# Off-diagonal blocks of the chunk inverses: four column groups of 32 instead of block-diagonal 128-wide products, with a new set of ordering numbers

## The chip, the cores and the metric

The kernel runs on one core of a Trainium2 chip. The metric is device time in microseconds (us) of one execution. The kernel before took 1522.41 us (median of 3 runs, 1519.56 to 1522.49). Engines are named as in the profile: PE multiplies matrices (PEld is its weight load), DVE, ACT and POOL work on vectors, SP issues the DMAs.

## What is computed

One layer of a hybrid decoder over 1024 prompt tokens and 8 sample tokens of width 1024: an input projection to 9360 columns, a gated linear attention branch (4 heads), an RWKV-7 branch (16 heads of 64), two up-projections merged by gates, an output projection, and a layer norm. The change lies in the RWKV-7 branch, whose recurrence is

```python
def step(S, inp):                       # S: [value, key] per head
    rt, wt, kt, vt, kkt, at = inp
    sa = jnp.einsum('bhvk,bhk->bhv', S, -kkt)
    S = S * wt[:, :, None, :] + sa[..., None] * (kkt * at)[:, :, None, :] + vt[..., None] * kt[:, :, None, :]
    y = jnp.einsum('bhvk,bhk->bhv', S, rt)
    return S, y
S, ys = lax.scan(step, S0, xs)
```

The projection around it is `p = jnp.einsum('btd,dn->btn', x, w_in)`, and the rest of the layer is

```python
m = (jax.nn.sigmoid(gate_a) * jnp.einsum('btc,cd->btd', o_gla, w_up_gla)
     + jax.nn.sigmoid(gate_b) * jnp.einsum('btc,cd->btd', o_rwkv, w_up_rwkv))
out = jnp.einsum('btd,de->bte', m, w_out)
y_out = _layernorm(DEEPNORM_ALPHA * x + out, ln_g, ln_b, LN_EPS)
```

## The kernel before

**Staging.** The prompt is handled in two passes of 512 tokens; the first also carries the 8 sample tokens. In each pass the weights stream by in blocks of 128 output columns (the big projections write the PSUM tile `proj`); each float32 product is made of three products in a rounded format (high by high, low by high, high by low: tiles `xh`, `xl` of the activations and `wpart` of the weights). Products between plain float32 tiles are recorded by the trace as two matmuls each, except transposes.

**One pair of heads.** The RWKV branch goes by pairs of heads, 8 in each pass, 16 in all. For a pair, `front` makes the chunk matrices: the 512 tokens are cut into `NCH = 8` chunks of `C = 64`, and for each chunk and head a unit-triangular 64 by 64 matrix has to be inverted. The two 32 by 32 diagonal blocks of each are inverted on POOL by 31 steps of elimination (tiles `X` and `Xt`; the operand comes back from DRAM as tile `wide<-LD`), written to DRAM (`XD`) and fetched into tile `XT` by DMAs. The off-diagonal block is (one diagonal inverse) times (the off-diagonal block of the matrix) times (the other diagonal inverse). `back` makes it in two products:

- Step one. Four DVE transposes bring one diagonal inverse of all 16 chunk-head blocks to tile `Xt` (128 partitions = 4 groups of 32, four blocks side by side). Tile `L1` (named `L` in the profile) has zeros but for one 32 by 32 block in each row group. Four matmuls of 128 by 128 weights and 32 moving columns write `pA`. Four copies of 32 partitions bring it to tile `As`, in blocks among zeros.
- Step two. Four matmuls with `As` as weights and 64 columns of `XT` write `pZ`; four copies put it into `XT`.

Then `turn` transposes some operands and `chain` walks through the 8 chunks with four dependent products each (PSUM tiles `pch` and `pY`).

**What sets the order.** Each activity (a pair, a head of the other branch, the block loop, the loads) is a Python generator that yields one instruction at a time. `Order.run` picks the next one by a table of costs (`price`), delays between engines (`HOP`, `SPARE`, `LANDED`), and precedences (`PRIO`, `FOR_PE`, `STAND`). Work that two engines can do goes to the one that the table says ends first, with penalties (`BIAS` for DVE against ACT, `ASIDE` for POOL). The result is one fixed order for each engine. `together` issues several matmuls as one piece. `KEEP` is how many free `row` tiles some requests must leave, and `AHEAD` is how many weight blocks before a change of activations the new activations begin to load. All matmuls, copies and DMAs are issued through the same helper, so nearly all rows of the profile bear L224.

PE can be used as one array (in the profile 128\*128, rows by columns), as two of 64 rows (64\*128: the products `big<-az,wide` in `front`), or as four groups of 32 columns (128\*32). Before, the last form is used only in `gla_sample`, for 8 products of the sample tokens with 256 moving columns, each on four groups (`big<-row 128*32`).

Of the kernel before, what the change touches and what calls it, by code (L numbers as in the profile page):

```python
# [20 lines left out]
P = 128  # L21
# [11 lines left out]
C = 64  # L33
# [15 lines left out]
    "Xt": ([P, P], 1), "S": ([P, GDV], 2), "Sp": ([P, C], 2), "s0p": ([P, C], 2), "rh": ([P, P], 2),  # L49
# [7 lines left out]
KEEP = 2  # L57
AHEAD = 3
# [6 lines left out]
SPARE_ROWS = 7  # L65
EARLY_GATES = 8


HOP = {"P": 0.2, "D": 0.26, "G": 0.14, "V": 0.14, "A": 0.14}
# [5 lines left out]
AGE = 0.5  # L75
# [3 lines left out]
BIAS = 0.145  # L79
ASIDE = 1.145  # L80

PRIO = {"evacuate": 0.7, "pair": 0.3, "turn": 0.5, "chain": 0.5, "norm": 0.1, "x": 0.56, "lora": 0.08, "rank":
        -0.15, "head": 0.3, "gate": -0.18, "w": 0.3, "out": -0.01, "state": 0.16, "block": 0.09}
FOR_PE = {"pair": 1.0, "turn": 1.11, "chain": 1.0, "norm": 0.76, "lora": 0.41, "rank": 1.0, "head": 1.0, "gate": 1.0,
        "state": 1.0, "out": 0.05}
STAND, SCARCE, PER_ROW = 0.042, 0.2, 0.036
# [63 lines left out]
def price(eng, name, out, args, ins):  # L150
# [277 lines left out]
class Kern(Order):  # L428
# [71 lines left out]
    def setup(self):  # L500
# [68 lines left out]

        for tag, n, bufs in (("az", 4 * HT, 2), ("XT", 2 * HT, 2), ("L1", HT, 1), ("As", HT, 1)):  # L570
# [556 lines left out]
    def front(self, c, p, st, d):  # L1127
# [118 lines left out]
        d.AZ, d.BK, d.G, d.XT, d.v, d.bonus, d.pc, d.L, d.L1 = AZ, BK, GG, XT, st[2], st[1], pc, L_, L1  # L1246
        d.y = Pc_[:, :HT]

    def back(self, d):
# [3 lines left out]
        As_, X1_ = (yield from self.get("As")), (yield from self.get("Xt"))  # L1253
        As = As_.rearrange("p (x t) -> p x t", t=P)
        X1 = X1_.rearrange("p (x t) -> p x t", t=32)
# [12 lines left out]
        pZ = yield from self.bank("big", [P, H, 2, 32])  # L1268
        for x in range(H):
            yield self.P.matmul(pZ[:, x], As[:, x], XT[:, x, :, 32:64], start=True, stop=True)  # L1270
        for h in range(2):
            for n in range(2):
                yield self.C.copy(XT[q[2 * h], H * n:H * n + H, h, 32:64], pZ[q[2 * h + n], :, h])
# [3 lines left out]
        self.free(pZ, As_)  # L1277
# [518 lines left out]
```

## Time and profile before

| What | us |
|---|---|
| Median of 3 runs | 1522.41 |
| The profiled execution | 1520.7 |
| Its span, first to last instruction | 1518.9 |
| PE busy | 1502.7 |
| PEld busy | 1348.3 |
| DVE busy | 1092.3 |
| ACT busy | 853.0 |
| POOL busy | 395.1 |

The mean granted clock of PE was 0.999. Rows of the grouped views read: line, engine, operation, output<-inputs, the array's form, partitions by elements, count, busy us, mean ns of one, and the idle time of the engine just before. Rows of the view in order of time read: start, duration, engine, operation, count, and in brackets the idle time before. A matmul's duration is its way through the array and overlaps those of its neighbours; what it costs the stream is the distance from its start to the next start.

### The profile page before, as it was taken

Reading aid. Unit: us, or ns where it says so; the run is one execution under the profiler, and the core shown is the slowest. Engines: PE = TensorE matmul, PEld = TensorE weight load, DVE = VectorE, ACT = ScalarE, POOL = GpSimd, SP = SyncE. Lnnn points to the kernel's source line nnn. Section 1 sums busy time; section 2 is a strip of 40 time slices with the busy share of each in tenths; the row PEclk is TensorE's granted clock in tenths of the full one; section 3 lists DMA queues with packets and bytes.
Section 4 is the critical chain, followed back from the end, with each engine's and each line's share of the span. In section 5 each row is a group of like instructions: output and inputs, shape, how many; then the busy total and the mean of one; then the engine's idle time right before and its main releaser. Section 6 shows DMA issues by size and latency. Waiting matters only on the chain.

```text
span 1518.9 us, 29410 instructions
## 1 busy us (share of the span) xinstructions
PE 1502.7 (99%) x10100; PEld 1348.3 (89%) x10100; DVE 1092.3 (72%) x2306; ACT 853.0 (56%) x2107; POOL 395.1 (26%) x1161
## 2 busy tenths in 40 slices
PE   9999999999999999999999999999999999999997
PEld 8899999999999998888888888888888898897786
DVE  6687596868786698757738695979577746675565
ACT  5556666676576566554746554465567645643210
POOL 2060516051503224052332505051451050000000
PEclk9999999999999999999999999999999999999999
DMA  8777776788677866664455456646574876786332
GB/s 297 261 266 239 269 228 222 239 273 263 203 239 255 289 225 191 217 204 138 153 173 166 126 178 198 207 127 219 181 219 142 247 246 230 260 273 205 128 112 84
DMA packets 206641, 318.45 MB, mean 210 GB/s; under 512 B 87075, under 2 KB 102572, under 8 KB 206492
## 3 DMA queue, kind: packets, MB, share of 16 engines
q1 hardware_dynamic: 206492, 316.56, 64.7%
q8 instruction: 81, 1.33, 0.3%
q14 instruction: 68, 0.56, 0.1%
HBM read 196.82 MB, written 118.61 MB: 208 GB/s over the span
## 4 chain that ended last, share of the span: by engine, by line
PE 94%; DVE 3%; DMA 1%; issue 1%; ACT 0%; SPq 0%; POOL 0%; POOLq 0%; DVEq 0%; ACTq 0%
PE proj L224 58%; PE big L224 21%; PE pY L224 9%; PE pch L224 6%; DVE row L224 1%; DMA wide<-LD 0%; DMA row<-o_gla 0%; DVE wide L224 0%; DVE wpart L224 0%; DVE xl L224 0%; DMA wraw<-w_in 0%; SPq L224 0%; DVE part L224 0%; ACT xh L224 0%; DVE pc L224 0%
## 5 line engine op out<-in xcount | busy, mean ns | idle before, releaser
L224 PE MATMUL proj<-xh,wpart 128*128 128x264 f32 (+2 forms) x3728 | 918.3, 329 | 1.0 <-DVE row L224 1.0
L224 PEld LDWEIGHTS proj<-xh,wpart 128*128 128x128 f32 x3728 | 623.1, 189 | 49.2 <-issue 4.2
L224 PE MATMUL proj<-xl,wpart 128*128 128x264 f32 (+2 forms) x1864 | 614.5, 330 | 0.4 <-DVE xl L224 0.4
L224 PEld LDWEIGHTS proj<-xl,wpart 128*128 128x128 f32 x1864 | 352.1, 189 | 22.2 <-DVE xl L224 1.7
L224 POOL TENSOR_TENSOR Xt<-X,wide 128x60 f32<-128x60 f32 (+24 forms) x496 | 163.7, 330 | 441.1 <-DMA wide<-LD 298.3
L224 DVE TENSOR_TENSOR wpart<-wraw,wpart 128x512 fp32r<-128x512 f32 x209 | 145.5, 698 | 73.4 <-ACT wpart L224 67.4
L224 ACT CAST wpart<-wraw 128x512 fp32r<-128x512 f32 x210 | 130.6, 623 | 98.7 <-PE proj L224 53.4
L224 DVE TENSOR_TENSOR row<-row 128x512 f32<-128x512 f32 (+10 forms) x331 | 173.3, 533 | 8.0 <-ACT row L224 2.2
L224 POOL TENSOR_TENSOR X<-X,Xt 128x60 f32<-128x60 f32 (+24 forms) x496 | 162.6, 328 | 38.8
L224 ACT ACTIVATE row<-row 128x512 f32<-128x512 f32 (+4 forms) x229 | 138.5, 612 | 29.0 <-DVE row L224 19.6
L224 ACT ACTIVATE s0p<-wide,pc 64x64 f32<-64x64 f32 x256 | 88.2, 345 | 34.6 <-DVE wide L224 30.0
L224 DVE SCALAR_TENSOR_TENSOR wide<-pch,pc,s0p 64x64 f32<-64x64 f32 x224 | 62.9, 281 | 59.9 <-PE pch L224 55.2
L224 ACT COPY wide<-pch 64x64 f32<-64x64 f32 x220 | 45.6, 207 | 107.3 <-PE pch L224 103.7
L224 POOL TENSOR_TENSOR row<-row 128x256 f32<-128x256 f32 (+4 forms) x38 | 36.3, 961 | 266.6 <-DVE row L224 187.6
L224 ACT ACTIVATE row<-proj,omu 128x256 f32<-128x256 f32 (+1 forms) x97 | 53.3, 550 | 73.6 <-PE proj L224 70.3
L224 DVE SCALAR_TENSOR_TENSOR row<-proj,pv,row 128x255 f32<-128x255 f32 (+1 forms) x97 | 55.6, 573 | 42.4 <-ACT tail L224 30.3
L224 PE MATMUL big<-row 128*128 128x128 f32 (+3 forms) x456 | 83.6, 314 | 0.0
L224 PE MATMUL big<-xh,wpart 128*128 128x256 f32 (+2 forms) x304 | 73.7, 327 | 0.6 <-ACT xh L224 0.6
L224 POOL TENSOR_SCALAR XT<-XT,st 128x256 f32<-128x256 f32 x1 | 1.2, 1227 | 272.7 <-ACT st L224 272.7
L406 ACT ACT_TABLE_LOAD x50 | 64.2, 1283 | 0.9
L224 DVE COPY rh<-pch 128x128 f32<-128x128 f32 x128 | 37.1, 290 | 37.2 <-PE pch L224 34.9
L224 PEld LDWEIGHTS big<-row 128*128 128x128 f32 (+2 forms) x456 | 58.8, 176 | 5.0 <-ACT row L224 0.6
(253 smaller groups left out, 2526.9 us busy)
## 6 DMA issues: line engine op xcount, KB each, us to landing
w<-wpart SPq DMA_DIRECT2D x146, 512.0 KB
wpart<-w SPq DMA_DIRECT2D x146, 512.0 KB
wraw<-w_in SPq DMA_DIRECT2D x146, 256.0 KB
wide<-LD SPq DMA_DIRECT2D x64, 128.0 KB
wraw<-w_up_gla SPq DMA_DIRECT2D x32, 256.0 KB
wraw<-w_up_rwkv SPq DMA_DIRECT2D x32, 256.0 KB
sg<-row SPq DMA_DIRECT2D x16, 260.0 KB
row<-sg SPq DMA_DIRECT2D x16, 260.0 KB
```

The source lines that it names most:

```text
L224: ways.append((eng, lambda call=call: call(out, *args, **kw), price(eng, name, out, args, ins)))
L406: self.nc.scalar.preload_act_table_set(self.table)
```

## The change

Both steps of `back` become four concurrent matmuls on four column groups of 32. In step one, the weights are the dense off-diagonal blocks (tile `Ld`, 32 columns for each group) and the moving operand is `Xd`, a tile of 512 columns with the transposed inverses in blocks among zeros; each group takes 128 moving columns. One copy of 128 by 128 brings `pA` to a tile out of `Xt`. In step two, this is the weights, 32 columns for each group, and the moving operand is `Yd`, the other diagonal inverses in blocks among zeros, 128 columns for each group. Four copies put `pZ` into `XT`, as before. The blocks of `Yd` come from DRAM by four DMAs of 16 KB, where two of 16 KB filled the off-diagonal part of `XT`. The four DMAs to `L1` go to `Ld`. The zeroed tiles are now `Yd` and `Xd` instead of `L1` and `As`; `Ld` (128 columns) is added.

The numbers that set the order are changed too: some precedences, penalties and delays, `KEEP` and `AHEAD`, and the price of a small product on column groups.

```diff
-KEEP = 2
-AHEAD = 3
+KEEP = 1
+AHEAD = 2
...
-SPARE_ROWS = 7
-EARLY_GATES = 8
+SPARE_ROWS = 8
+EARLY_GATES = 9
...
-BIAS = 0.145
-ASIDE = 1.145
+BIAS = 0.203
+ASIDE = 1.644
...
-        return 0.1365 if cols == P else 0.142 if rows == P else 0.95
+        return 0.1365 if cols == P else (0.142 if n > P else 0.074) if rows == P else 0.95
...
-        L1 = (yield from self.get("L1")).rearrange("p (x t) -> p x t", t=P)
+        Ld_, Yd_ = (yield from self.get("Ld")), (yield from self.get("Yd"))
+        Ld = Ld_.rearrange("p (x t) -> p x t", t=32)
+        Yd = Yd_.rearrange("p (g x t) -> p g x t", g=4, t=32)
...
-                g, to = 2 * h + n, 2 * h + 1 - n
-                yield self.S.dma_start(L1[32 * g:32 * g + 32, :, 32 * to:32 * to + 32],
-                                       GG[64 * h:64 * h + 32, H * n:H * n + H, 0, h, 32:64])
+                g = 2 * h + n
+                yield self.S.dma_start(Ld[32 * g:32 * g + 32], GG[64 * h:64 * h + 32, H * n:H * n + H, 0, h, 32:64])
...
-        for h in range(2):
-            yield self.S.dma_start(XT[64 * h:64 * h + 32, 0:H, h, 32:64],
-                                   XD[(2 + h) * NCH + H:(3 + h) * NCH].rearrange("c s t -> s c t"))
+        for x in range(H):
+            yield self.S.dma_start(Yd[32 * x:32 * x + 32, :, x], XD[2 * NCH + x:4 * NCH:H].rearrange("g s t -> s g t"))
...
-                yield self.V.transpose(X1[q[2 * h + n]], XT[q[2 * h], H * n:H * n + H, h, 0:32])
-        pA = yield from self.bank("big", [P, H, 32])
-        for x in range(H):
-            yield self.P.matmul(pA[:, x], d.L1[:, x], X1[:, x], start=True, stop=True)
-        for h in range(2):
-            for n in range(2):
-                g = 2 * h + 1 - n
-                yield self.C.copy(As[q[g], :, q[2 * h + n]], pA[q[g]])
-        self.free(pA, X1_, d.L1)
-        pZ = yield from self.bank("big", [P, H, 2, 32])
-        for x in range(H):
-            yield self.P.matmul(pZ[:, x], As[:, x], XT[:, x, :, 32:64], start=True, stop=True)
+                g = 2 * h + n
+                yield self.V.transpose(Xd[q[g], :, g], XT[q[2 * h], H * n:H * n + H, h, 0:32])
+        pA = yield from self.bank("big", [P, P])
+        yield together([self.P.matmul(pA[q[x]], d.Ld[:, x * 32:x * 32 + 32], Xd_[:, x * P:x * P + P], start=True, stop=True)
+                        for x in range(H)])
+        As = yield from self.get("Xt")
+        yield self.C.copy(As, pA)
+        self.free(pA, Xd_, d.Ld)
+        pZ = yield from self.bank("big", [P, P])
+        yield together([self.P.matmul(pZ[q[g]], As[:, g * 32:g * 32 + 32], d.Yd[:, g * P:g * P + P], start=True, stop=True)
+                        for g in range(4)])
+        pZ3 = pZ.rearrange("p (x t) -> p x t", t=32)
```

Three places show how instructions stand before and after. In the rows, `xNN` behind the sizes counts equal instructions in a row; `proj<-xh` and `proj<-xl` are projections of the block loop, and their tile numbers only tell which eighth of the activations they read.

PE in the first pair, before: step one is `big<-Xt,L`, step two `big<-XT,As`, and `big<-az,wide` are the 64-row products of the next pair's `front`.

```order
L224 MATMUL proj<-xl_262,wpart 128x256
L224 MATMUL big<-Xt,L_187 128x32 x4
L224 MATMUL big<-az_180,wide 128x128 x8
L224 MATMUL proj<-xh_253,wpart 128x256
...
L224 MATMUL big<-XT_183,As_189 128x64 x4
L224 MATMUL big<-az_180,wide 128x128 x8
L224 MATMUL proj<-xh_355,wpart 128x256
```

PE in the first pair, after: the same place, with step one `big<-Xd,Ld` and step two `big<-Yd,Xt`.

```order
L224 MATMUL proj<-xl_260,wpart 128x256
L224 MATMUL big<-Xd_189,Ld 32x128 x4
L224 MATMUL proj<-xh_251,wpart 128x256
L224 MATMUL proj<-xh_259,wpart 128x256
L224 MATMUL proj<-xl_313,wpart 128x256
L224 MATMUL big<-az_180,wide 128x128 x8
L224 MATMUL big<-Yd_187,Xt 32x128 x4
L224 MATMUL proj<-xh_259,wpart 128x256
```

Each step is still four matmuls, now 32 output partitions by 128 columns, and it stands between projections of the full array, or next to the 64-row products.

PE in the ninth pair, the first of the second pass, before: from step one to step two.

```order
L224 MATMUL big<-Xt,L_187 128x32 x4
L224 MATMUL proj<-xh_8907,wpart 128x512
L224 MATMUL proj<-xh_8915,wpart 128x512
L224 MATMUL proj<-xl_8926,wpart 128x512
L224 MATMUL proj<-xh_8915,wpart 128x512
L224 MATMUL proj<-xh_8932,wpart 128x512
L224 MATMUL proj<-xl_8934,wpart 128x512
L224 MATMUL proj<-xh_8932,wpart 128x512
L224 MATMUL proj<-xh_8939,wpart 128x512
L224 MATMUL proj<-xl_8950,wpart 128x512
L224 MATMUL big<-XT_183,As_189 128x64 x4
```

PE in the ninth pair, after: from step one to step two.

```order
L224 MATMUL big<-Xd_189,Ld 32x128 x4
L224 MATMUL proj<-xh_9172,wpart 128x512
L224 MATMUL proj<-xl_9185,wpart 128x512
L224 MATMUL proj<-xh_9172,wpart 128x512
L224 MATMUL proj<-xh_9184,wpart 128x512
L224 MATMUL proj<-xl_9201,wpart 128x512
L224 MATMUL big<-Yd_187,Xt 32x128 x4
```

Nine projections stood between the two steps, and now five.

SP's DMA queue in the second pair, before: the diagonal inverses go to `XT` (32x8x32, four DMAs), then the part of step two (32x4x32); `wraw` is a load of weights, `w` a store of split weights.

```order
L224 DMA XT_184<-XD_2747 32x8x32 x3
L224 DMA wraw<-w_in 128x512
L224 DMA w_0_2880<-wpart 128x1024
L224 DMA XT_184<-XD_2747 32x8x32
L224 DMA XT_184<-XD_2747 32x4x32 x2
L224 DMA wraw<-w_in 128x512
L224 DMA w_1_2927<-wpart 128x1024
```

SP's DMA queue in the second pair, after.

```order
L224 DMA XT_184<-XD_2749 32x8x32 x4
L224 DMA Yd_187<-XD_2749 32x4x32
L224 DMA wraw<-w_in 128x512
L224 DMA w_0_2905<-wpart 128x1024
L224 DMA Yd_187<-XD_2749 32x4x32 x2
L224 DMA o_gla<-row 128x520
L224 DMA wraw<-w_in 128x512
L224 DMA w_1_2946<-wpart 128x1024
L224 DMA o_gla<-row 128x520
L224 DMA Yd_187<-XD_2749 32x4x32
```

The operands of step two are now four DMAs, and they stand in three pieces, with weights and a result of the other branch between them.

Over the whole program PE has 8783 matmuls before and after; 32 more DMAs are issued on SP (1329 for 1297); ACT has 12 copies fewer; 29 elementwise products go from POOL to DVE, and DVE has 35 copies fewer.

More of the change, by code (lines that the diff above doesn't have):

```diff
@@ L64 @@
 RANKW, RANKM = 48, 66
[L65 to L69 removed]
+SPARE_ROWS = 8
+EARLY_GATES = 9
+HOP = {"P": 0.2, "D": 0.26, "G": 0.12, "V": 0.14, "A": 0.14}
 SWITCH = 0.074
@@ L73 @@
 TABLE = 1.28
-AGE = 0.5
+AGE = 0.648
 SPARE = 0.4
 LANDED = 0.605
-BIAS = 0.145
-ASIDE = 1.145
-PRIO = {"evacuate": 0.7, "pair": 0.3, "turn": 0.5, "chain": 0.5, "norm": 0.1, "x": 0.56, "lora": 0.08, "rank":
-        -0.15, "head": 0.3, "gate": -0.18, "w": 0.3, "out": -0.01, "state": 0.16, "block": 0.09}
+BIAS = 0.203
+ASIDE = 1.644
+PRIO = {"evacuate": 0.7, "pair": 0.3, "turn": 0.31, "chain": 0.5, "norm": 0.11, "x": 0.96, "lora": 0.21, "rank":
+        -0.15, "head": 0.3, "gate": -0.18, "w": 0.3, "out": 0.15, "state": 0.16, "block": 0.17}
 FOR_PE = {"pair": 1.0, "turn": 1.11, "chain": 1.0, "norm": 0.76, "lora": 0.41, "rank": 1.0, "head": 1.0, "gate": 1.0,
         "state": 1.0, "out": 0.05}
-STAND, SCARCE, PER_ROW = 0.042, 0.2, 0.036
+STAND, SCARCE, PER_ROW = 0.074, 0.307, 0.036
 URGENT = 0.767
@@ L567, in setup @@
         nc.vector.memset(self.reset[:, ::C], 0)
-        for tag, n, bufs in (("az", 4 * HT, 2), ("XT", 2 * HT, 2), ("L1", HT, 1), ("As", HT, 1)):
+        for tag, n, bufs in (("az", 4 * HT, 2), ("XT", 2 * HT, 2), ("Yd", HT, 1), ("Xd", HT, 1)):
             ts = [cp.tile([P, n], F32, name=f"{tag}{i}") for i in range(bufs)]
@@ L1252, in back @@
         H = NCH // 2
-        As_, X1_ = (yield from self.get("As")), (yield from self.get("Xt"))
-        As = As_.rearrange("p (x t) -> p x t", t=P)
-        X1 = X1_.rearrange("p (x t) -> p x t", t=32)
+        Xd_ = yield from self.get("Xd")
+        Xd = Xd_.rearrange("p (x g t) -> p x g t", g=4, t=32)
         q = [slice(32 * n, 32 * n + 32) for n in range(4)]
```

8 lines of the change are left out of this document (4 added, 4 removed).

## The prediction

> **What bounds the kernel now.** I read the page's busy times and its chain first, then the stretches, then what PE waited for.
>
> ```profile
> PE 1502.7 (99%) x10100; PEld 1348.3 (89%) x10100; DVE 1092.3 (72%) x2306; ACT 853.0 (56%) x2107; POOL 395.1 (26%) x1161
> PE 94%; DVE 3%; DMA 1%; issue 1%; ACT 0%; SPq 0%; POOL 0%; POOLq 0%; DVEq 0%; ACTq 0%
> ```
>
> PE is busy for 99% of the span, and 94% of the chain that ended last is PE. Busy time alone could flatter PE, since matmuls overlap, so I looked at where it stood idle.
>
> ```profile
> 0.00:25.00 25.00, 22.36 (x155) 21.17 (x156) 16.48 (x42) 13.96 (x30) 7.70 (x17) 1.00 0.94 345
> 125.00:600.00 475.00, 474.12 (x3961) 460.77 (x3960) 361.99 (x803) 313.89 (x848) 152.08 (x440) 1.00 0.73 242
> 600.00:1200.00 600.00, 597.37 (x3404) 503.78 (x3403) 446.92 (x970) 345.34 (x848) 186.47 (x575) 1.00 0.59 180
> 1420.00:1519.00 99.00, 91.33 (x418) 73.73 (x416) 56.30 (x90) 9.35 (x26) 2.77 (x3) 0.98 0.27 91
> ```
>
> The columns are the stretch, its length, busy us of PE, PEld, DVE, ACT and POOL, then clock, DMA share and GB/s. In the 1075 us from 125 to 1200, where all pairs but the last lie, PE is idle for 3.5 us. The large loss is at the end (7.7 us, the last rows' normalisation), which the change does not touch. The clock is full. So a microsecond less of PE's stream is worth nearly a microsecond of the whole, if the new order opens no gaps, and little else can be won: only some 8.6 us of idle time that the page shows lie outside the end (16.3 us between the span and PE's busy time, less 7.7).
>
> **Term 1: the two steps on PE.** What a step costs is the time that it pushes the projections apart. In the fourth pair both steps stand alone between projections; first step one, then step two:
>
> ```profile
> 364.77 0.28 PE L224 MATMUL proj<-xl,wpart 128*128 128x264 f32 x1
> 364.89 0.41 PE L224 MATMUL proj<-xh,wpart 128*128 128x264 f32 x2
> 365.14 0.97 PE L224 MATMUL big<-Xt,L 128*128 128x32 f32 x8
> 365.94 0.37 PE L224 MATMUL proj<-xl,wpart 128*128 128x264 f32 x1
> 366.15 0.40 PE L224 MATMUL proj<-xh,wpart 128*128 128x264 f32 x2
> 366.38 0.28 PE L224 MATMUL proj<-xl,wpart 128*128 128x256 f32 x1
> ...
> 368.17 0.28 PE L224 MATMUL proj<-xl,wpart 128*128 128x256 f32 x1
> 368.28 0.28 PE L224 MATMUL proj<-xh,wpart 128*128 128x256 f32 x1
> 368.40 1.00 PE L224 MATMUL big<-XT,As 128*128 128x64 f32 x8
> 369.21 0.36 PE L224 MATMUL proj<-xh,wpart 128*128 128x256 f32 x1
> 369.41 0.28 PE L224 MATMUL proj<-xl,wpart 128*128 128x256 f32 x1
> ```
>
> Two projections take 0.23 us (366.15 to 366.38), so one takes 0.12. From 364.77 to 366.15 are 1.38 us with four projections: step one costs 1.38 - 0.48 = 0.90 us. From 368.17 to 369.41 are 1.24 us with three: step two costs 1.24 - 0.36 = 0.88 us. Neither is sized by its 32 or 64 moving columns: eight recorded matmuls at 0.11 us each make 0.88.
>
> The new form has a near relative, the four-group products of the sample tokens:
>
> ```profile
> 148.69 0.39 PE L224 MATMUL pch<-wide,gg 128*128 128x128 f32 x2
> 148.91 0.39 PE L224 MATMUL pY<-az,wide 128*128 128x128 f32 x2
> 149.23 0.64 PE L224 MATMUL big<-row 128*32 128x256 f32 x8
> 149.80 0.52 PE L224 MATMUL proj<-xh,wpart 128*128 128x264 f32 x2
> 150.16 0.38 PE L224 MATMUL pch<-rh,XT 128*128 128x128 f32 x2
> ```
>
> From 148.91 to 150.16 are 1.25 us. The `pY` product takes 0.22 (148.69 to 148.91) and two projections 0.24, so four groups of 256 columns cost 0.79 us, with the change of the array's form before and after. The four groups do run together: eight recorded matmuls of 256 columns start and make room for the next projection within 0.57 us (149.23 to 149.80). The change streams 128 columns instead. The full-array pair of these two widths shows what that saves:
>
> ```profile
> 118.45 0.39 PE L224 MATMUL big<-row,S 128*128 128x128 f32 x2
> 118.68 0.59 PE L224 MATMUL big<-row 128*128 128x256 f32 x2
> ```
>
> 0.59 - 0.39 = 0.20 us for the two passes. A new step therefore costs 0.79 - 0.20 = 0.59 us, and a pair saves 0.90 + 0.88 - 2 x 0.59 = 0.60 us. Sixteen pairs: 16 x 0.60 = 9.6 us. In two places the order puts a step next to other products of a divided array (the first pair's step two follows the 64-row products); whether a form change is saved there I leave at nothing, with 0.1 us each as the bound. For a step's bounds: if changing the form cost nothing, two passes of 0.11 us would be left and a step would save 0.67, 21 us in all; if the four groups did not overlap at 128 columns, eight at 0.11 and the 0.37 of the form changes (0.59 - 0.22) would make 1.25 us, a loss of 0.36 per step and 11.5 us in all. I take 0.59, because its row has the same array form, element type and number of groups and differs only in width.
>
> The Trainium skill speaks to both ends. Its page TensorEngine Tiling (Array Packing), section Theoretical Speedup, gives up to 4 times for a dimension of at most 32, which would turn 0.90 into an estimated 0.22 and the sum into some 21 us. The same page, section Key Properties, says that a change of mode drains the engine, and the row at 149.23, 0.32 us after a product that takes 0.22, agrees with that.
>
> **Term 2: the copies and the POOL work that moves.** ACT and DVE are not the bound, so these count through waits only.
>
> ```profile
> L224 ACT COPY As<-big 32x128 f32<-32x128 f32 x58 | 14.9, 257 | 20.7 <-PE big L224 20.1
> L224 ACT COPY row<-big 128x128 f32<-128x128 f32 x64 | 14.2, 269 | 18.8 <-PE big L224 18.5
> L224 POOL TENSOR_TENSOR Xt<-X,wide 128x60 f32<-128x60 f32 (+24 forms) x496 | 163.7, 330 | 441.1 <-DMA wide<-LD 298.3 <-DVE wide L224 34.0 <-DMA wraw<-w_in 27.8
> L224 DVE TENSOR_TENSOR row<-row 128x512 f32<-128x512 f32 x125 | 88.6, 712 | 3.9 <-ACT row L224 1.2 <-POOL Xt L224 1.1
> ```
>
> Four copies of 257 ns between the steps become one of about 269, so step two can start 0.76 us sooner after step one, and ACT is 12 us lighter over the kernel. DVE takes 29 products from POOL, at most 0.71 us each or 21 us, and loses 35 copies; at 72% busy it has room for that on average. The copy also adds a wait: its target is now `Xt`, in which POOL's elimination works (31 products of 0.33 us into it per pair and as many sums, some 20 us). If the next pair's elimination held it, step two and all of PE behind it would stand. In the order after at most 4 us of PE's work lie between the two steps, by these durations, so no elimination fits in. I count nothing for all this. The cover is the projections that stand between dependent products; if it is gone, DVE is late in front of PE, as at 684 us:
>
> ```profile
> 684.34 0.73 DVE L224 SCALAR_TENSOR_TENSOR row<-proj,pv,row 128x511 f32<-128x511 f32 x1
> 685.13 1.24 DVE L224 STREAM_TRANSPOSE Xt<-XT 32x128 f32<-32x128 f32 x4
> 686.47 1.05 PE L224 MATMUL big<-Xt,L 128*128 128x32 f32 x8 [1.70 <-issue]
> ```
>
> That is the longest of PE's waits: step one stood behind transposes that DVE had reached late, 1.7 us. The transposes stay four per pair, now with strided writes; at worst they double and push step one by 1.2 us, where DVE is late already; at best nothing.
>
> In the ninth pair five projections of 0.23 us are left between the steps, 1.2 us. What must fit in is the tail of the products, a copy and its signal. Here is that sequence where DVE made the copies:
>
> ```profile
> 1025.12 1.19 DVE L224 COPY As<-big 32x128 f32<-32x128 f32 x4
> 1026.41 0.85 PE L224 MATMUL big<-XT,As 128*128 128x64 f32 x6
> ```
>
> PE started 0.10 us after the last copy. With about 0.28 for the last product's way through the array (0.39 for a pair less 0.11), 0.27 for the copy and 0.10, some 0.65 us are needed; 0.5 us remain, less than one long ACT instruction. I price this at nothing, with 0.3 us for each of 16 pairs, 5 us, as the far end.
>
> **Term 3: DMAs.** Two more DMAs of a pair, all on SP, behind weights.
>
> ```profile
> 674.54 1.57 SPq L224 DMA_DIRECT2D XT<-XD  x3
> 676.21 0.40 SPq L224 DMA_DIRECT2D wpart<-w  x1
> 676.71 0.38 SPq L224 DMA_DIRECT2D sg<-row  x1
> 677.13 1.56 SPq L224 DMA_DIRECT2D XT<-XD  x3
> 678.79 16.46 SPq L224 DMA_DIRECT2D wpart<-w  x5
> ```
>
> One costs SP 0.52 us, 32 make 17 us, of a queue that spends long in waits (five weight loads take 16.5 us here, since they wait for free tiles). SP is in order, so whatever stands behind a waiting weight load waits 3.3 us with it. Step two now needs four DMAs where it needed two, but they have the transposes (1.24 us) and step one to land behind. I count nothing; the far end is in the rivals.
>
> **Term 4: the order set anew.** `AHEAD` = 2 gives the next activations two weight blocks, each 24 projections of 0.23 us (5.6 us), so 11 us instead of 17 to load. `KEEP` = 1 lets rows be taken sooner. No row prices these. The upper bound of a gain is the 8.6 us of visible idle time; a loss of the same size is as easy to imagine. I take zero, and 8 us both ways for the range.
>
> **Sum.** 9.6 us from term 1, nothing from the others: the profiled execution, 1520.7 us, becomes 1511.1. The median of the runs shown is 1.7 us above that execution, and by it the sum is 1512.8. I forecast 1512.
>
> **Rivals.** *The form changes cost nothing:* the bound of 21 us comes true, 1522.4 - 21 = 1501. Against it stands the row at 149.23. The Trainium skill's factor of four, named above, is the rule for this case. *The new order closes gaps:* with most of the 8.6 us of idle time gone as well, 1522.4 - 9.6 - 7 = 1506; nothing in the trace speaks for it, and little against. *Late operands turn the sign:* the four DMAs to `Yd` are cut by weights in the queue in ten of the pairs. If the last piece comes one weight wait late (3.3 us) where about 2.8 us of transposes, step one and projections lie ahead (1.24 + 0.35 + 1.2), each such pair loses some 0.5 us, 5 us; from 1 us of wait in each of ten pairs on, the gain is gone, and at the full 3.3 us the loss is 33 - 9.6, or 1546. At 1.5 us, which I would hold likeliest in this case, 1522.4 - 9.6 + 15 = 1528. Against it: in the rows at 674 and 677 the `XT` transfers are cut in the same way, and PE's waits have no DMA as a cause. *The time moves into gaps:* DVE, with 29 products more, is late in front of PE as at 684, six times 1.7 us: 1523, no change. *The groups do not overlap at 128 columns:* 1522.4 + 11.5 = 1534; the row at 149.23 speaks against it.
>
> **From this to the numbers.** Three runs lie within 0.2% (1519.56 to 1522.49), and I call less than 0.2% no change, that is 1519.4 to 1525.4. Chances: the forecast, 1507 to 1517, 0.64; form changes for nothing 0.03; gaps closed, below 1507, 0.09; a smaller gain, 1517 to 1519.4, 0.06; no change by gaps 0.09; late operands 0.07; no overlap 0.02. Faster is 0.64 + 0.03 + 0.09 + 0.06 = 0.82, same 0.09, slower 0.09. The range leaves out the slower cases, most of the unchanged ones and the lowest of the fast ones: 1503 to 1520 holds about 0.8.
>
> **What would show it.** In the profile after: groups `big<-Xd,Ld` and `big<-Yd,Xt` on 128\*32 that push the projections apart by 0.5 to 0.65 us each (term 1); one copy of about 0.27 us in front of step two, and PE waits for ACT there of no more than 0.3 us (term 2); no PE wait for a DMA at step two (term 3); PE's idle time outside the end between 5 and 14 us (term 4). I am wrong if a step costs 0.8 us or more, or if PE's waits grow by about 10 us.

## The result, and the profile after

The change makes the kernel slower. Its median is 1530.32 us (six runs, 1527.35 to 1534.67), that of the kernel before 1522.36 us (six runs, 1519.4 to 1525.11). The ratio is 1.0053, with a 95% interval of 1.0032 to 1.0075. I had forecast 1512.

The profiled execution took 1532.67 us, with a span of 1530.9; before it was 1518.9. First the page's busy times and its chain of work, after the change:

```profile
PE 1501.6 (98%) x10100; PEld 1329.8 (87%) x10100; DVE 1094.8 (72%) x2296; ACT 851.9 (56%) x2100; POOL 370.6 (24%) x1130
PE 39%; DMA 2%; SPq 2%; DVE 0%; issue 0%; ACT 0%; POOL 0%; POOLq 0%; ACTq 0%
```

PE's busy time fell by 1.1 us only, where the products alone should have taken some 10 us from it (matmuls that run at half clock, shown below, count as busy for longer). The chain can't be used here as it was before: its shares add up to 43%, so it was followed over less than half of the span. The stretches show where the idle time is (columns as in the prediction):

```profile
125.00:600.00 475.00, 472.15 (x3991) 454.65 (x3991) 372.75 (x816) 323.28 (x877) 138.53 (x417) 1.00 0.74 243
600.00:1200.00 600.00, 588.03 (x3301) 482.89 (x3300) 430.30 (x929) 328.53 (x797) 175.85 (x563) 0.99 0.57 174
1420.00:1531.00 111.00, 103.27 (x469) 83.53 (x468) 64.42 (x103) 14.78 (x34) 2.77 (x3) 0.98 0.32 109
```

From 125 to 1200 us PE is idle for 14.8 us (2.85 + 11.97) instead of 3.5. The end still loses 7.7 us. And the mean granted clock of the second stretch is 0.99 instead of 1.00. What PE waited for, after the change:

```profile
PE big L224 <- DMA Yd<-XD: 8.1, 5, 2.8
PE big L224 <- DVE Xd L224: 4.7, 4, 1.9
PE big L224 <- issue: 1.4, 1, 1.4
...
PE big L224 <- DMA o_gla<-row: 1.1, 1, 1.1
...
PE big L224 <- ACT row L224: 0.6, 1, 0.6
```

The columns are the sum in us, the number of waits and the longest. The waits for `Yd` are new: no wait of PE had a DMA as its cause before. With the `issue`, `o_gla` and `row` rows, which also stand in front of step two, step two waits 11.2 us in 8 of the 16 pairs. Step one waits for `Xd`, DVE's transposes, 4.7 us instead of the one 1.7 us of before. Most of that is not DVE's own work: before these transposes DVE in turn stands for the transfers to `XT`, which it never did before the change. The view of DVE's waits has

```profile
DVE Xd L224 <- DMA XT<-XD: 6.7, 5, 2.4
```

and the eleventh pair shows how it reaches PE (three of step one's four waits, 4.4 us of the 4.7, end on such a transpose):

```profile
863.26 0.62 DVE L224 STREAM_TRANSPOSE Xd<-XT 32x128 f32<-32x128 f32 x2 [1.72 <-DMA XT<-XD]
863.94 0.43 PE L224 MATMUL big<-Xd,Ld 128*32 128x128 f32 x8 [1.78 <-DVE Xd L224]
```

The steps themselves did what was forecast. Step one of the fourth pair, after:

```profile
352.64 0.40 PE L224 MATMUL proj<-xh,wpart 128*128 128x264 f32 x2
352.98 0.42 PE L224 MATMUL big<-Xd,Ld 128*32 128x128 f32 x8
353.33 0.39 PE L224 MATMUL proj<-xl,wpart 128*128 128x256 f32 x1
353.56 0.40 PE L224 MATMUL proj<-xh,wpart 128*128 128x256 f32 x2
```

From 352.64 to 353.56 are 0.92 us with three projections of 0.12: the step costs 0.56 us. By the same reading its median over the pairs is 0.56 us, and that of each old step 0.89. The two steps of 16 pairs save 32 x 0.33, or some 10.6 us.

The largest wait, in the twelfth pair, shows how step two comes to stand. SP's queue first, then PE, both after the change:

```profile
951.37 1.12 SPq L224 DMA_DIRECT2D XT<-XD  x2
952.53 0.45 SPq L224 DMA_DIRECT2D wpart<-w  x1
953.02 0.92 SPq L224 DMA_DIRECT2D XT<-XD  x2
953.99 1.40 SPq L224 DMA_DIRECT2D Yd<-XD  x3
955.49 0.38 SPq L224 DMA_DIRECT2D wpart<-w  x1
955.91 0.43 SPq L224 DMA_DIRECT2D Yd<-XD  x1
```

```profile
954.82 0.43 PE L224 MATMUL big<-Xd,Ld 128*32 128x128 f32 x8
955.18 0.50 PE L224 MATMUL proj<-xh,wpart 128*128 128x512 f32 x1
955.51 0.40 PE L224 MATMUL proj<-xl,wpart 128*128 128x512 f32 x1
955.75 0.79 PE L224 MATMUL proj<-xh,wpart 128*128 128x512 f32 x2
959.35 0.66 PE L224 MATMUL big<-Yd,Xt 128*32 128x128 f32 x8 [2.81 <-DMA Yd<-XD]
959.93 0.80 PE L224 MATMUL proj<-xl,wpart 128*128 128x512 f32 x1
960.52 1.06 PE L224 MATMUL proj<-xh,wpart 128*128 128x512 f32 x2
961.38 0.63 PE L224 MATMUL proj<-xl,wpart 128*128 128x512 f32 x1
961.80 0.63 PE L224 MATMUL proj<-xh,wpart 128*128 128x512 f32 x1
```

No waiting weight load cut the four DMAs here; each weight load between them took SP only 0.4 us. SP needed from 951.37 to 956.34 to issue all eight, the last `Yd` after step one had started, and step two could start 3.0 us after that last issue had ended. PE had four projections to fill it. The Trainium skill, page DMA: Bandwidth & Descriptors, section Anatomy of one DMA, puts a fixed cost of some 2.0 us on a transfer of GpSimd's path, most of it the receipt of the last write. The transfers here are SP's, and their 3.0 us are of that order and longer, at a time when the DMA engines were 90% busy (the window at 956.30 below).

Behind the wait the projections are slow: from 959.93 to 960.52 one takes 0.59 us, and from 961.38 to 961.80 one takes 0.42, where 0.23 is usual. The windows around it give the granted clock (the third number from the end of a row):

```profile
940.00:950.00 10.00, 10.00 (x45) 8.11 (x44) 8.23 (x13) 5.19 (x9) 4.44 (x11) 1.00 0.30 78
956.30:959.30 3.00, 0.23 (x1) 0.00 (x0) 2.97 (x7) 0.53 (x2) 0.00 (x0) 0.96 0.90 300
959.30:962.10 2.80, 2.75 (x13) 1.97 (x14) 2.58 (x5) 1.03 (x4) 0.00 (x0) 0.50 0.94 312
962.10:970.00 7.90, 7.90 (x58) 6.23 (x58) 4.04 (x8) 2.64 (x6) 2.87 (x7) 0.98 0.32 116
```

For 2.8 us after the wait PE had half its clock. That is most of a stretch from 959.03 to 962.44; between 30 us and the last 10 us there are three more, one at 798.61 (shown in the last section) and these:

```profile
1105.81:1112.64 6.83, 6.00 (x23) 4.58 (x24) 6.09 (x12) 1.93 (x7) 0.00 (x0) 0.50 0.55 158
1273.06:1276.47 3.41, 3.41 (x12) 2.71 (x11) 1.50 (x3) 2.21 (x7) 0.00 (x0) 0.50 0.94 262
```

Each of the four begins within 0.9 us of the end of a wait of step two for `Yd` (the waits end at 798.74, 959.35, 1106.64 and 1272.25). The kernel before has no such stretch between 30 us and its last 10.

I added these up over the whole of the two profiled executions (PE's starts, row by row; half clock is what projections took above their usual time where several in a row took 1.7 times as long or more). Span after less span before is 12.0 us. The steps, with the form change behind them, make it 10.9 us shorter. Waits that the trace names grew by 12.4 us, the time lost at half clock by 5.5 (0.8 to 6.3), and 5.0 us are left in stalls too short for the trace to name. The last two can't be told apart well. The kernel before has no half clock there, so its 0.8 us are the error of this way of adding up; and in the four stretches of the change PE was busy 15.8 us, of which half, 7.9 us, may be lost, with 2.6 left for the short stalls.

### The profile page after: what moved, and what is told of

Same layout as the page of the kernel before. It is cut to its first block, busy times and chain, and to the rows that moved or that the text cites. A ratio compares the mean times of both kernels' runs of the same rounds, so it can differ in the third digit from the quotient of the medians.

```text
span 1530.9 us, 29363 instructions
## 1 busy us (share of the span) xinstructions
PE 1501.6 (98%) x10100; PEld 1329.8 (87%) x10100; DVE 1094.8 (72%) x2296; ACT 851.9 (56%) x2100; POOL 370.6 (24%) x1130
## 5 line engine op out<-in xcount | busy, mean ns | idle before, releaser
L224 PE MATMUL proj<-xh,wpart 128*128 128x256 f32 (+2 forms) x3728 | 919.9, 330 | 1.2 <-DVE row L224 1.0
L224 PE MATMUL proj<-xl,wpart 128*128 128x256 f32 (+2 forms) x1864 | 615.4, 330 | 0.0
L224 DVE TENSOR_TENSOR row<-row 128x512 f32<-128x512 f32 (+10 forms) x357 | 185.5, 531 | 10.1 <-ACT row L224 3.2
L224 ACT COPY wide<-pch 64x64 f32<-64x64 f32 x237 | 49.1, 207 | 117.9 <-PE pch L224 112.6
L224 POOL TENSOR_TENSOR row<-row 128x256 f32<-128x256 f32 (+1 forms) x12 | 13.7, 1142 | 255.7 <-DVE row L224 160.6
L224 PE MATMUL big<-xh,wpart 128*128 128x264 f32 (+2 forms) x288 | 70.9, 329 | 0.0
L224 ACT ACTIVATE row<-proj 128x128 f32<-128x128 f32 (+4 forms) x136 | 37.1, 325 | 44.8 <-PE proj L224 44.5
```

The costliest lines, as they stand in the source:

```text
L224: ways.append((eng, lambda call=call: call(out, *args, **kw), price(eng, name, out, args, ins)))
```

## The experiments

I began with two theories. **A:** step two stands for late `Yd` transfers, and the half clock behind each long stand comes on top. **B:** the new ordering numbers cost the time, whatever the products. Later came **C:** any re-set order of this program costs waits until its numbers are searched for it. "Steps' distance" below is the median over the pairs of the time from the start of step one to that of step two, less the wait in front of step two; it was 2.98 us before and 1.71 after the change.

### Products and numbers apart

The new products with the ordering numbers of before:

```diff
-KEEP = 1
-AHEAD = 2
+KEEP = 2
+AHEAD = 3
...
-AGE = 0.648
+AGE = 0.5
...
-STAND, SCARCE, PER_ROW = 0.074, 0.307, 0.036
+STAND, SCARCE, PER_ROW = 0.042, 0.2, 0.036
```

> The new products with all ordering numbers of before (only the price of a small product on column groups stays new). Theory A, step two stands for its Yd transfers and the PE clock drops after each long stand: the planner prices these transfers as before, so step two again waits in several pairs; 1520 to 1530 us, and the granted clock below 0.998. Theory B, the new numbers cost the time by waits elsewhere: without them the 10 us of the products are won, 1510 to 1514 us.

Measured: 1551.13 us (1547.01 to 1557.08), ratio 1.0185 (1.0162 to 1.0208); neither theory's range holds it. Step two waits 9.1 us. PE's named waits are 35.7 us after the first 30, against 5.9 before; one of them, 12.3 us long, is a projection standing for ACT's `xh`.

The products of before with the new numbers (the same lines the other way round):

> The products of before with all new ordering numbers. Theory A: no Yd, so no wait for it; 1518 to 1526 us, as before. Theory B: the numbers bring their loss with them, 20 us of it were needed to turn a gain of 10 into a loss of 8; 1535 to 1545 us.

Measured: 1535.97 us (1532.15 to 1536.61), ratio 1.008 (1.0065 to 1.0095). That is theory B's range. Step two waits for nothing here, and yet 13.5 us are lost. So the numbers of before don't fit the new products (21 us worse than the new ones), and the new ones don't fit the old products: B is right that they cost time there. But with the old numbers the new products are slower still, so the numbers alone don't explain the loss.

### Telling the planner that Yd comes late

In the changed kernel the planner counts `Yd` as landed 1.5 us later:

```diff
             yield self.S.dma_start(Yd[32 * x:32 * x + 32, :, x], XD[2 * NCH + x:4 * NCH:H].rearrange("g s t -> s g t"))
+        at, by = self.ready[Yd_.tensor.name]
+        self.ready[Yd_.tensor.name] = at + 1.5, by
```

> The changed kernel, with Yd held to land 1.5 us later by the planner, which then puts step two later among the projections in the pairs where it believed it close. Theory A: PE's waits for Yd shrink from 8.1 us to under 4 us, clock above 0.996; 1516 to 1524 us. Theory B: no change, 1528 to 1533 us.

Measured: 1532.8 us (1528.48 to 1542.23), ratio 1.0076 (1.0051 to 1.0102), where A had said 1516 to 1524 and B 1528 to 1533. Step two now waits 1.2 us in place of 11.2. But all named waits together are 20.5 us, where they were 17.8: step one stands for DVE's transposes (once for 3.3 us, while DVE stands 3.7 us for `XT`), other products for DVE's `row` and ACT's `wide`. Step two's waits went, and the time did not: waits came up in other places.

### Other work between the steps

The 12 transposes on PE that `turn` makes (8 of `BK`, 4 of `v`, with their copies) are issued between the two steps instead of behind them; nothing else changes:

```diff
         yield from self.back(d)
-        yield from self.turn(d)
...
         self.free(pA, Xd_, d.Ld)
+        yield from self.turn(d)
         pZ = yield from self.bank("big", [P, P])
```

> The changed kernel, with the 12 transposes of turn issued between the two steps instead of behind them, so that 4 to 6 us of PE's work lie between the steps in every pair. Theory A: no PE wait for Yd is left, clock 0.998 or more, and the 10 us of the products show: 1508 to 1516 us. Theory B: 1528 to 1533 us.

Measured: 1515.61 us (1514.81 to 1520.25, six runs), ratio 0.9956 (0.9941 to 0.997). This beats both kernels, and lies in A's range. The steps' distance is 4.94 us. The twelfth pair of this version, SP's queue and then PE:

```profile
936.26 2.81 SPq L224 DMA_DIRECT2D Yd<-XD  x4
```

```profile
937.73 0.42 PE L224 MATMUL big<-Xd,Ld 128*32 128x128 f32 x8
938.08 0.50 PE L224 MATMUL big<-part,headsr 128*128 128x512 f32 x1
938.42 0.60 PE L224 MATMUL big<-cons,wide 128*128 128x128 f32 x4
...
942.29 0.39 PE L224 MATMUL proj<-xh,wpart 128*128 128x512 f32 x1
942.61 0.42 PE L224 MATMUL big<-Yd,Xt 128*32 128x128 f32 x8
942.97 0.50 PE L224 MATMUL proj<-xh,wpart 128*128 128x512 f32 x1
943.30 0.40 PE L224 MATMUL proj<-xl,wpart 128*128 128x512 f32 x1
```

The last `Yd` is issued at 939.07 (936.26 + 2.81), 1.3 us after step one has started, much as in the change; but step two comes 3.5 us later, with PE full, and no wait stands beside it. (From 942.29 to 943.30 less two projections of 0.23 are 0.55 us: what step two costs.) In the whole run step two waits for nothing, step one waits 1.0 us, DVE stands 0.7 us for `XT` instead of 6.7, and between 30 us and the last 10 us one stretch of 3.41 us is left at half clock (from 600.82), which may cost half its length.

### The same order without the late operand

The order of the change is kept, but the four DMAs of each pair write a spare tile, so that step two has no transfer to wait for. The spare tile is one more 128 x 128 tile:

```diff
-            yield self.S.dma_start(Yd[32 * x:32 * x + 32, :, x], XD[2 * NCH + x:4 * NCH:H].rearrange("g s t -> s g t"))
+            op = self.S.dma_start(Yd[32 * x:32 * x + 32, :, x], XD[2 * NCH + x:4 * NCH:H].rearrange("g s t -> s g t"))
+            to = self.spare.rearrange("p (g t) -> p g t", g=4)[32 * x:32 * x + 32]
+            fn = lambda x=x, to=to: self.nc.sync.dma_start(to, XD[2 * NCH + x:4 * NCH:H].rearrange("g s t -> s g t"))
+            op.ways = [("S", fn, op.cost)]
+            op.fn = fn
+            yield op
```

> The changed kernel instruction for instruction, but the four DMAs that should fill Yd write to a spare tile, so step two does not wait for them; Yd stays zero, and the off-diagonal blocks of the inverses come out as zeros. Theory A, the late transfers and the half clock behind them are the loss: PE's waits for Yd (8.1 us) and most of the stretches at half clock go; 1512 to 1520 us. Theory C, the loss is spread over the order, and other operands end the waits a moment later: 1524 us or more.

Measured: 1523.62 us (1519.26 to 1527.7, twelve runs), ratio 1.0001 (0.999 to 1.0013). A had said 1512 to 1520, C 1524 or more; it lies between. From PE's and from DVE's waits in this version:

```profile
PE big L224 <- DVE Xd L224: 3.9, 4, 2.0
```

```profile
DVE Xd L224 <- DMA XT<-XD: 6.4, 5, 2.0
```

Every instruction of PE, DVE, ACT and POOL stands in the same order as in the change. Step two's waits are gone, also those that the trace had put down to `issue`, `o_gla` and ACT's `row`, so these were waits for `Yd` too; and the median falls by 6.7 us, or by 7.7 where each is taken against the kernel before that ran beside it (8.0 and 0.3 us above it). That settles A as a cause, and also that `Yd` isn't the whole: with 10.6 us saved on the steps, 1511.8 was to be had, and 11 to 12 us are still missing.

Some of that has late transfers behind it as well. Step one still stands for transposes, 3.7 of its 3.9 us while DVE stands for `XT`, whose transfers this version keeps. And two stretches at half clock are left, with PE busy throughout, some 3.4 us lost:

```profile
861.11:864.52 3.41, 3.41 (x25) 2.08 (x17) 2.04 (x6) 0.89 (x3) 0.00 (x0) 0.50 1.05 321
1212.69:1216.10 3.41, 3.41 (x18) 3.41 (x17) 1.17 (x3) 1.11 (x5) 1.56 (x7) 0.50 0.55 170
```

The first follows a wait of step one of 1.96 us, up to 860.90. (The profiled execution is the fastest of the twelve, 13.4 us below that of the change; I go by the medians.)

### Room between the steps by the old order

The new products, the numbers of before, and a planner told the costs of the old form (steps 0.888 us, the copy 1.4, a `Yd` transfer 0.28, the copy's target taken first), so that the order comes close to that of before:

```diff
-        yield together([self.P.matmul(pA[q[x]], d.Ld[:, x * 32:x * 32 + 32], Xd_[:, x * P:x * P + P], start=True, stop=True)
-                        for x in range(H)])
...
-        yield self.C.copy(As, pA)
+        pA = yield from self.bank("big", [P, P])
+        yield planned(together([self.P.matmul(pA[q[x]], d.Ld[:, x * 32:x * 32 + 32], Xd_[:, x * P:x * P + P], start=True, stop=True)
+                        for x in range(H)]), 4 * 0.222)
+        yield planned(self.C.copy(As, pA), 1.4)
```

> The new products with the ordering numbers of before, and the planner told that the two steps, the copy and the transfers cost what they did before, so that step two stays some 2.5 us of PE's work behind step one, as before. Theory A: few waits for Yd, the products' 10 us show; 1510 to 1518 us. Theory C, any new order of this program costs 5 to 20 us of waits until its numbers are searched for it: 1520 to 1540 us, with the waits at other operands.

Measured: 1533.42 us (1530.71 to 1535.92), ratio 1.0068 (1.0054 to 1.0082). The steps' distance is 2.87 us, almost that of before; step two waits 2.9 us, and yet the named waits are 18.4 us. They lie at other products, and behind two of them, of 0.87 and 1.37 us up to 1193.83, the clock is halved from 1194.26 to 1204.50. A alone cannot explain that; C's range holds the time.

### Does any new order cost?

`turn` between the steps, with all numbers of before (the change of place shown above, the numbers as in the first experiment):

> turn between the two steps, new products, ordering numbers of before. Theory A: no wait for Yd, so within 5 us of the same with the new numbers (1515.6), 1511 to 1521 us. Theory C: its own waits, 1520 to 1540 us.

Measured: 1529.23 us (1526.71 to 1530.42), ratio 1.0039 (1.0026 to 1.0051): C's range. No wait at step two, named waits 15.7 us.

The kernel before with `turn` between its old steps:

```diff
         yield from self.back(d)
-        yield from self.turn(d)
...
+        yield from self.turn(d)
         pZ = yield from self.bank("big", [P, H, 2, 32])
```

> The kernel before, old products and numbers, with turn between the two steps. It tells whether that move is a gain by itself. Theory A: step two of before did not wait, so nothing is won; 1519 to 1526 us. Theory C: a new order without a search, 1526 to 1540 us.

Measured: 1542.38 us (1541.84 to 1547.03), ratio 1.0135 (1.0119 to 1.0151). Named waits 17.1 us, none at step two. So the same move gains 14.7 us where step two has a late operand and loses 20 us where it has none. The gain is about twice the 6.7 to 7.7 us that came of taking `Yd`'s transfers away. In the profile the move also did away with most of the waits for `XT`; what that is worth, and what is left to the order, no run takes apart.

Then one number only. In the kernel before, GpSimd's signal, and in a second kernel the weight of age:

```diff
-HOP = {"P": 0.2, "D": 0.26, "G": 0.14, "V": 0.14, "A": 0.14}
+HOP = {"P": 0.2, "D": 0.26, "G": 0.12, "V": 0.14, "A": 0.14}
```

> The kernel before with one number of the planner changed (GpSimd's signal 0.12 instead of 0.14 us); nothing else. 404 lines of PE's order differ, from the eleventh pair or so on. If any re-set order costs waits until its numbers are searched for it (theory C): 1525 to 1540 us, with PE's waits after 30 us grown from 5.9 to 9 or more. If the order only costs where operands come late from a DMA (theory A), there is nothing here for it to act on: 1520 to 1525 us.

Measured: 1522.63 us (1519.78 to 1528.68, eleven runs), ratio 0.9998 (0.9984 to 1.0011): no change.

```diff
-AGE = 0.5
+AGE = 0.53
```

> The kernel before with one other number of the planner changed (AGE 0.53 instead of 0.5); 8585 lines of PE's order differ. Theory C: 1527 to 1545 us, more than with 404 lines. Theory A: 1520 to 1525 us.

Measured: 1525.19 us (1522.8 to 1529.04, eleven runs), ratio 1.0009 (0.9999 to 1.002). Although this one moves thousands of rows, it costs about a thousandth at most. C as I had put it, for any re-set order, falls.

The same number put back in the changed kernel, and in the version with `turn` between:

```diff
-HOP = {"P": 0.2, "D": 0.26, "G": 0.12, "V": 0.14, "A": 0.14}
+HOP = {"P": 0.2, "D": 0.26, "G": 0.14, "V": 0.14, "A": 0.14}
```

> The changed kernel with one number put back (GpSimd's signal 0.14 instead of 0.12 us). 11189 lines of PE's order differ; step two still stands close behind step one. Theory A: the late Yd transfers stay, so 1526 to 1536 us. Theory C: the changed kernel's numbers fit it no better than any, so it scatters by 10 us to either side, 1520 to 1545.

Measured: 1536.66 us (1529.09 to 1539.16, five runs), ratio 1.0074 (1.0049 to 1.0099), with 10.5 us of waits at step two. That is just above A's range and inside C's wide one, so it tells little between them.

> The products of the change with the transposes of turn between the steps, and the same one number put back (0.14 instead of 0.12 us). If the room between the steps is what made that version faster (theory A): 1513 to 1520 us, PE's waits for Yd still nothing. If it was a lucky order (theory C): 1520 to 1535.

Measured: 1517.38 us (1515.42 to 1519.48, six runs), ratio 0.9963 (0.9947 to 0.9979), with 0.5 us of waits at step two. That is A's range. The gain of the moved transposes is no luck of one order. It comes out under three sets of numbers (medians of different sets of runs; that of the kernel before lay between 1522.4 and 1524.0 in them):

| numbers | `turn` behind step two | `turn` between the steps | difference |
|---|---|---|---|
| new | 1530.32 | 1515.61 | -14.7 |
| new, one put back | 1536.66 | 1517.38 | -19.3 |
| of before | 1551.13 | 1529.23 | -21.9 |
| of before, products of before | 1522.36 | 1542.38 | +20.0 |

### Which of the numbers

The new numbers cost the old products 13.5 us. Only the four that rule how early rows and loads are taken:

```diff
-KEEP = 2
-AHEAD = 3
+KEEP = 1
+AHEAD = 2
...
-SPARE_ROWS = 7
-EARLY_GATES = 8
+SPARE_ROWS = 8
+EARLY_GATES = 9
```

> The products of before; of the new numbers only the four that say how early rows and loads are taken (KEEP 1, AHEAD 2, SPARE_ROWS 8, EARLY_GATES 9); 7930 lines of PE's order differ. All the new numbers cost the products of before 13.5 us. If the new numbers cost by too little room for loads and rows, most of it is here: 1530 to 1538 us, with the new waits of PE at the heads of blocks, on splits and loads. If it is the priorities: 1521 to 1526.

Measured: 1542.07 us (1540.81 to 1543.92), ratio 1.0122 (1.0105 to 1.0139), more than was expected. Only the priorities, ages and delays (the other lines of the change's block from `HOP` to `STAND`):

> The other half: products of before, KEEP, AHEAD, SPARE_ROWS and EARLY_GATES of before, all priorities, ages and delays new; 15032 lines of PE's order differ. If the priorities cost: 1530 to 1538 us, with PE's new waits on DVE's small results (part, S, gg). If the room costs: 1521 to 1526. If both halves only fit each other (a set searched as a whole), both kernels are slower than the 1536 us of all the new numbers, or about as slow.

Measured: 1532.48 us (1530.86 to 1535.33), ratio 1.0059 (1.0044 to 1.0074). The stretches from 600 and from 1200 us of the first, then those from 125 us of the second:

```profile
600.00:1200.00 600.00, 591.74 (x3316) 496.43 (x3315) 422.46 (x912) 331.37 (x805) 195.13 (x587) 1.00 0.58 174
1200.00:1420.00 220.00, 211.78 (x1375) 190.34 (x1374) 143.91 (x272) 121.67 (x251) 23.68 (x62) 0.98 0.70 228
```

```profile
125.00:600.00 475.00, 469.94 (x3922) 456.54 (x3921) 371.68 (x823) 315.77 (x858) 145.58 (x431) 1.00 0.73 236
600.00:1200.00 600.00, 596.14 (x3396) 499.72 (x3395) 443.73 (x956) 345.78 (x835) 169.76 (x556) 1.00 0.60 179
1200.00:1420.00 220.00, 218.56 (x1389) 195.86 (x1389) 135.14 (x255) 114.43 (x231) 23.44 (x62) 1.00 0.77 244
```

With the four numbers of room PE idles 16.5 us in the 820 us from 600 on, where the kernel before idles 5.1; with the priorities 5.3 there, no more than before, and 5.1 from 125 to 600, where the kernel before loses 0.9. Each half costs, and the room alone costs more than both halves together (19 against 13.5 us). So what a set of these numbers costs is not the sum of its parts.

The version that wins, `turn` between the steps with the new products, but with the four of before:

```diff
-KEEP = 1
-AHEAD = 2
+KEEP = 2
+AHEAD = 3
...
-SPARE_ROWS = 8
-EARLY_GATES = 9
+SPARE_ROWS = 7
+EARLY_GATES = 8
```

> The products of the change with turn between the steps; new priorities, but KEEP, AHEAD, SPARE_ROWS and EARLY_GATES of before. With all the new numbers it took 1515.6 us, with all of before 1529.2. If the room matters: 1512 to 1520 when more room is only a help, 1520 to 1532 when the four new numbers carry the gain. If the priorities carry it: 1514 to 1519.

Measured: 1521.88 us (1516.95 to 1525.48, ten runs), ratio 0.9989 (0.9975 to 1.0002). Two of its waits, 3.6 us together, are projections standing for a weight load. That is the range in which the four new numbers carry the gain: they are worth 6.3 us here (5.5 against the kernel before run beside each), with the opposite sign to the old products. The runs of this version spread over 8.5 us.

## Why the prediction was wrong

**Term 1 was right,** and a little small: I gave 0.59 us per step and 9.6 us in all; measured are 0.56 and some 10.6. The groups do run together at 128 columns, and changing the form costs: the projection behind the step at 353.33 takes 0.23 us where 0.12 is usual. The Trainium skill's rule that a change of mode drains the engine (page TensorEngine Tiling (Array Packing), section Key Properties) agrees with those 0.11 us. The estimate of 21 us by its factor of four does not come true.

**Term 2 was right.** One copy of 0.27 us stands between the steps. The one wait that the trace puts down to ACT in front of step two (0.6 us, where I allowed 0.3) is gone when `Yd`'s transfers are. No elimination on POOL held `Xt`: none of ACT's 15 copies into it waited for POOL. Step one did wait more for the transposes, 4.7 us in place of 1.7, but 4.4 of them belong to the next term.

**Term 3 failed,** at the sentence that the transfers "have the transposes (1.24 us) and step one to land behind". I counted the DMAs by their price on SP and assumed that they were on their way when the transposes began. They stand behind all of `XT` in the same queue: in the twelfth pair the issue of the last began at 955.91, while step one started at 954.82. Their time to land, 3.0 us from the end of that issue, had no term at all, and the order had cut the steps' distance from 2.98 to 1.71 us. What I held against the rival "late operands" was that the `XT` transfers were cut in the same way and PE never waited for a DMA. That was no evidence: PE does not read those transfers before step two, DVE's transposes do, and the two that step two did read had 3 us. After the change `XT` was late as well, 6.7 us in front of DVE, 4.4 of them passed on to step one. Why `XT` lands late in the new order and not in the old one, no run takes apart.

The rival's sum was 1528, and its wait of 1.5 us per pair came close (11.2 us in eight pairs are 1.4 each), in part by luck: it expected ten such pairs, and the cause was SP's issue and the landing, not a waiting weight load (in the pairs where step two waited, none between the pieces of `Yd` took SP more than 0.5 us). It also lacked a term: the half clock behind the long waits, 5.5 to 7.9 us more in the profiled execution.

**Term 4 failed in part, and how far stays open.** "I take zero, and 8 us both ways": with step two's transfers taken away, 11 to 12 us of the products' gain are still missing. Not all of it is the order's own. In the profile of that version 3.7 us of step one's waits come of late `XT` transfers, and some 3.4 us are lost at half clock; about 4 us sit in stalls too short to be named. That profile is of the fastest of its runs, 4.4 us below their median, and no trace stands for those 4.4 us. That the rest was lost to the order is inferred from that remainder. On the products of before, the new numbers cost 13.5 us by direct measurement. I had the wrong bound as well: visible idle time limits what an order can gain, but not what it can lose.

**The sum:** 1522.4 - 10.6 (the steps) + 6.7 (late `Yd` and the half clock that went with it, by the spare-target version) + 11.8 (the remainder) = 1530.3. The last term makes it come out, is measured only as that remainder, and holds the late `XT`.

Of the signs that I named, the steps' cost came true; the PE wait for a DMA at step two, and PE's idle time outside the end (21.6 us, that is 1530.9 - 1501.6 - 7.7, where I said 5 to 14), both went against me. So did the growth of PE's waits by about 10 us that I had named as a sign of being wrong: they grew by 12.4.

## What to carry to other kernels

When a step that multiplies gets cheaper, look at what its operands' last transfer needs from issue to landing, and where in the queue that issue stands, and not only at what the transfer costs the queue: the distance between dependent steps must hold that time, and independent work of the same engine (here 12 transposes) moved between them turned a loss of 0.5% into a gain of 0.4%. Without a late operand the same move cost 1.3%. Price an order that is set anew with a loss of its own, since its numbers may fit one program: in the kernel before, a change of one number cost at most 0.1%, a foreign set 0.8%, and one half of that set 1.2%. Where the clock halves behind a wait, the wait costs more than its length: here 1.51 us of waiting brought 3.41 us at half clock.

## What was not expected of the hardware

PE's clock halves after quite short waits. Two places of the changed kernel: behind a wait of 1.51 us, up to 798.74, and around two waits of 1.78 and 1.45 us, up to 863.94 and 867.10.

```profile
795.20:798.61 3.41, 1.55 (x12) 0.83 (x12) 3.34 (x8) 0.56 (x2) 0.00 (x0) 1.00 0.88 266
798.61:802.02 3.41, 3.28 (x15) 2.36 (x16) 3.35 (x7) 1.03 (x4) 0.00 (x0) 0.50 0.64 181
863.46:866.87 3.41, 1.71 (x15) 1.05 (x15) 2.69 (x8) 0.75 (x2) 0.00 (x0) 1.00 0.85 254
866.87:870.28 3.41, 3.19 (x26) 2.70 (x27) 1.50 (x3) 2.62 (x6) 0.00 (x0) 1.00 0.81 260
```

The first wait halved the clock for 3.41 us; the other two, longer together, did not touch it. So the length alone does not decide. The trace shows more: the four stretches at half clock last 3.41 us or twice that, and their starts (798.61, 959.03, 1105.81, 1273.06) lie 160.42, 146.78 and 167.25 us apart, that is 47, 43 and 49 times 3.413 us, so they stand on one grid. In this execution they also sort by how long PE was busy in the 3.41 us before: 1.55, 0.91, 1.54 and 1.28 us ahead of the four, and 1.71 us from 863.46, behind which nothing happened. That is no sharp border (in the version with the spare target 2.23 us were followed by half clock at 1212.69), and PE's busy time is modelled.

The Trainium skill, page TensorE: Matmul & The Clock Gate, section Part 1: The HAM clock gate, says half rate comes after an idle window of some 3.4 us which runs freely, without regard to the kernel. The grid of 3.41 us agrees with the window's length, and a window that runs freely would explain that one wait hits and another doesn't. But the windows ahead of the four stretches were not idle throughout, since PE was busy for up to 1.55 us of them; here the measurement decides.

The six executions of the change show what it is worth: three at a mean granted clock of 0.996 to 0.997 took 1527.35 to 1527.97 us, and three at 0.991 to 0.993 took 1532.67 to 1534.67, the profiled one among them. The spread of this kernel goes with its granted clock.
